# A decoder block with a grouped mixture of experts: h2 kept in natural column order, its first parts made later, slot weights by float32r products

## The chip, the cores and the metric

The kernel runs on one core of one Trainium2 chip. Its time is device microseconds for one execution of the whole program; several executions are made and the median counts. All tensors are float32 in HBM.

## The reference

One decoder layer on 256 tokens of 1024 columns. A mixing part (two kinds of attention, two gated branches, an output projection) makes a new residual `x`. Then a router picks for every token one group of four and two experts in it, out of 16 experts of width 512:

```python
h2 = rmsnorm(x, norm2_g[l]) * (1.0 + scale2) + shift2
...
g_prob = jax.nn.softmax((hf @ rg_w + rg_b).astype(jnp.float32), axis=-1)
g_top_p, g_idx = lax.top_k(g_prob, 1)
...
for e in range(N_EXPERTS):
    act = jax.nn.silu(hf @ w_gate[e]) * (hf @ w_up[e])
    out = out + combine[:, e:e + 1] * (act @ w_down[e])
```

The residual `x + gate2 * moe(h2)` is normalised once more and is the output.

## The kernel before

The mixing part fills the first half of the time; the change does not touch it. The second half works as follows.

**Router.** Tokens stand on partitions in two tiles `t` (128 tokens each), the 1024 columns in two halves `n`. `wo_steps` makes the output projection on TensorE, `x1_half(t, n)` turns one of its four quarters into the new residual (three VectorE operations, L947, L948 and L950) and sums squares on ScalarE (L949). `rstd2` makes the factor of the norm on GpSimd. `q_transpose` turns the tile (L956, copied by ScalarE, L957), `token_logits` multiplies it with the router's weights, `fold` copies the sums (L908) and adds them up, `weigh_logits` finishes the logits. Nineteen small VectorE and TensorE steps follow (`larger`, `place`, `selb`, the rank `rk`), `mod_rows(5)` puts two plain float32 products on TensorE, and `one_hot` writes, for each expert, a 0/1 matrix of 128 tokens by 64 slots.

**h2.** `h2_half` finishes h2 in place (L997). `h2_hi` rounds a half to float32r on ScalarE (L1009) and `h2_lo` takes the rest on VectorE (L1012); the pair of parts keeps float32 accuracy in float32r products. Both read h2 at every fourth column, because the expert weights lie in SBUF with rows `4p+k` on partition `p`: they read strided and write a permuted tile, whose 128 columns `k` stand together.

**Gather.** `gather(g, half)` runs once for each of the four groups: for eight column blocks `k`, the parts of h2 of two token tiles are the stationary operand (128x128) and the one-hot matrix of four experts (256 columns) is the moving one. That is 32 products for a group (L1200), in float32r.

**Experts.** Pairs `p` = 0 to 7. For a pair TensorE does gate and up products (`in_half`, L1240), then `slot_weights(p)`, then the down products of the pair before (`down_rows`, L1297) with `act_transpose` between their halves. `scatter_pair` (L1331) adds the result of pair `p-2` into the residual, with the transposed one-hot matrix `sT` as stationary operand. `slot_weights` before: two transposes of the one-hot matrix through TensorE (L1250), two plain float32 products with the combine weights (16 columns, L1252), a ScalarE copy of the transposed matrix (L1255) and two of the weights `ws` (L1258).

**Order.** In the router TensorE, VectorE and ScalarE run in the order in which the code is written (`manual_schedule`), and in the expert loop TensorE does. In the loop a scheduler sets the order on the other engines. The expert weights, some 100 MB, come over SyncE's queue into ring buffers; a load waits until the tile that had its buffer is used up.

Of the kernel before, what the change touches and what calls it, by code (L numbers as in the profile page):

```python
# [61 lines left out]
def hybrid_block_kernel(  # L62
# [931 lines left out]
    def h2_half(t, n):  # L994

        cs = slice(512 * n, 512 * n + 512)
        V.scalar_tensor_tensor(h2[t][:, cs], h2[t][:, cs], r2[t], adaacc[3, n], op0=ALU.mult,  # L997
                               op1=ALU.add)

    def h2_cols(t, n):  # L1000

        return h2[t][:, 512 * n:512 * n + 512].rearrange("t (p k) -> t k p", k=4)

    def h2_part(t, i, n):
        return h2s[t][i][:, 512 * n:512 * n + 512].rearrange("t (k p) -> t k p", k=4)

    def h2_hi(t, n):

        S.copy(h2_part(t, 0, n), h2_cols(t, n))  # L1009

    def h2_lo(t, n):
        V.tensor_tensor(h2_part(t, 1, n), h2_cols(t, n), h2_part(t, 0, n).bitcast(F32),  # L1012
                        op=ALU.subtract)

    def tok(t):
        return slice(t * P, (t + 1) * P)
# [13 lines left out]
    rstd2(0)  # L1030
    q_transpose(0, 0)
    h2_half(0, 0)
    h2_hi(0, 0)
    h2_lo(0, 0)
    wo_steps(1, ws, [(k, 1) for k in W3])
    q_transpose(0, 1)
    q_transpose(1, 0)
    token_logits(0)
    seed(0, 0)
    fold(tok(0), 0, "lgs0")  # L1040
    x1_half(1, 1)
    rstd2(1)
    q_transpose(1, 1)
    seed(0, 1)
    weigh_logits(0)
    h2_half(0, 1)
    h2_half(1, 0)
    token_logits(1)
    fold(tok(1), 32, "lgs1")
# [5 lines left out]
    seed(1, 0)  # L1055
    seed(1, 1)

    larger = moe.tile([P, SETS, 16], F32, name="larger", bufs=1)
    G.memset(larger, 0.0)

    def rt(shape, name, dt=F32):
# [126 lines left out]
    def gather(g, half):  # L1188

        if half == 0:  # L1190
            hgs[g] = late.tile([P, KD, 4 * CAP], F32, name="hg", tag="s8", bufs=2)
        hg, oh = hgs[g], onehot[g % 2]
        for k2 in range(2 * half, 2 * half + 2):
            ps = psa(f"hg{g}{k2}")
            for kk in range(2):
                k = 2 * k2 + kk
                n = 0
                for t in range(NT):
                    for i in range(2):
                        PE.matmul(ps[:, kk * T:(kk + 1) * T], h2s[t][i][:, k * P:(k + 1) * P],  # L1200
                                  oh[:, t].rearrange("p e s -> p (e s)"),
                                  start=(n == 0 and kk == 0), stop=(n == 3), skip_group_check=True)
                        n += 1
            S.copy(hg[:, 2 * k2:2 * k2 + 2, :], ps.rearrange("p (k s) -> p k s", k=2))
# [39 lines left out]
    def slot_weights(p):  # L1244

        lo = (2 * p) % 4
        oh = [onehot[p // 2 % 2][:, t, lo:lo + 2, :].rearrange("p e s -> p (e s)") for t in range(NT)]
        sp = psa(f"st{p}")
        for t in range(NT):
            PE.transpose(sp[:, t * P:(t + 1) * P], oh[t].bitcast(F32), ident)  # L1250
        for t in range(NT):
            PE.matmul(sp[:, T:T + NE], oh[t].bitcast(F32), combv[:, t, :], start=(t == 0),  # L1252
                      stop=(t == 1))
        sT = moe.tile([P, T], F32R, name="sT", tag="sT")
        S.copy(sT, sp[:, 0:T])  # L1255
        ws = moe.tile([P, 1], F32, name="ws", tag="ws")
        for i in range(2):
            S.copy(ws[64 * i:64 * i + 64, :],  # L1258
                   sp[64 * i:64 * i + 64, T + 2 * p + i:T + 2 * p + i + 1])
        sw[p] = ws, sT  # L1260

    def silu_up(p):
# [60 lines left out]
        V.tensor_tensor(yl, y, hi.bitcast(F32), op=ALU.subtract)  # L1323
        ys[p, FW * n] = hi, yl

    def scatter(yy, sT, n, cs):

        for y in yy:
            for t in range(NT):
                m = sT[:, t * P:(t + 1) * P]  # L1330
                PE.matmul(oacc[t][n][:, cs], m.bitcast(F32) if len(yy) == 1 else m, y, start=False,  # L1331
                          stop=True, skip_group_check=True)

    def scatter_pair(p, n, c):
        scatter(ys.pop((p, c.start)), sw[p][1], n, slice(c.start - FW * n, c.stop - FW * n))

    one_hot(0)
    for t in range(NT):
        h2_lo(t, 1)
    combv = route_weights()  # L1340
    by_hand.__exit__(None, None, None)
    NP = NE // 2
    whole_cols = [slice(0, FW), slice(FW, D)]
# [56 lines left out]
    with tc.If(nmaxv > CAP):  # L1400
        iota2 = small.tile([P, P], F32, name="iota2", tag="lgs")
        G.iota(iota2, pattern=[[1, P]], base=1, channel_multiplier=0,
               allow_small_or_imprecise_dtypes=True)
        with tc.For_i(0, NE, 1) as e:
            def load(w, name):
                hs = []
                for i in range(2):
                    h = w.shape[1] // 2
                    t_ = ring.tile([P, 2048], F32, name=f"{name}{i}", tag="ring")
                    k = h // P  # L1410
                    tv = t_.rearrange("p (k f) -> p k f", k=k)
                    src = w[bass.ds(e, 1), i * h:(i + 1) * h, :]
                    nc.sync.dma_start(tv, src.rearrange("a (p k) f -> p (a k) f", k=k) if k == 4 else
                                      src.rearrange("a (k p) f -> p (a k) f", p=P))
                    hs.append(tv)
                return hs
            gw, uw, dw = load(w_gate, "og"), load(w_up, "ou"), load(w_down, "od")
            pe_ = moe.tile([P, NT], F32, name="pe_")
            ce_ = moe.tile([P, NT], F32, name="ce_")
            for t in range(NT):  # L1420
                V.tensor_copy(pe_[:, t:t + 1], pos[:, t, bass.ds(e, 1)])
                V.tensor_copy(ce_[:, t:t + 1], combv[:, t, bass.ds(e, 1)])
            for r0 in (CAP, CAP + P):
                pr = moe.tile([P, NT], F32, name="pr")
                V.tensor_scalar(pr, pe_, float(-r0), None, op0=ALU.add)
                so = yhs[1][:, 0:NT * P].rearrange("p (t s) -> p t s", t=NT)
                for t in range(NT):
                    V.tensor_scalar(so[:, t, :], iota2, pr[:, t:t + 1], None, op0=ALU.is_equal)
                hq = late.tile([P, KD, P], F32, name="hq", tag="s8", bufs=2)
                for k in range(KD):  # L1430
                    ps = psa("ohg")
                    for n, (t, i) in enumerate(((0, 0), (0, 1), (1, 0), (1, 1))):
                        PE.matmul(ps[:, 0:P], h2s[t][i][:, k * P:(k + 1) * P], so[:, t, :],
                                  start=(n == 0), stop=(n == 3))
                    S.copy(hq[:, k, :], ps[:, 0:P])
                sp = psa("ost")
                for t in range(NT):
                    PE.transpose(sp[:, t * P:(t + 1) * P], so[:, t, :].bitcast(F32), ident)
                sT = moe.tile([P, T], F32R, name="osT", tag="sT")
                S.copy(sT, sp[:, 0:T])  # L1440
                wp = psa("owp")
                for t in range(NT):
                    PE.matmul(wp[:, 0:1], so[:, t, :].bitcast(F32), ce_[:, t:t + 1],
                              start=(t == 0), stop=(t == 1))
                ws = moe.tile([P, 1], F32, name="ows", tag="ws")
                V.tensor_copy(ws, wp[:, 0:1])
                gu = []
                for nm, hs in (("og", gw), ("ou", uw)):
                    ps = psa(f"{nm}ps")
                    for k in range(KD):  # L1450
                        PE.matmul(ps, hq[:, k, :], hs[k // 4][:, k % 4, :], start=(k == 0),
                                  stop=(k == KD - 1))
                    gu.append(ps)
                S.activation(act, gu[0], AF.Silu)
                V.tensor_tensor(act, act, gu[1], op=ALU.mult)
                ap = psa("oactT")
                for f in range(KF):
                    PE.transpose(ap[:, f * P:(f + 1) * P], act[:, f * P:(f + 1) * P], ident)
                aT = moe.tile([P, KF, P], F32, name="oaT", tag="aT")
                V.tensor_copy(aT, ap.rearrange("p (f s) -> p f s", f=KF))  # L1460
                for n in range(2):
                    cs = slice(512 * n, 512 * n + 512)
                    ps = psa("odps")
                    for f in range(KF):
                        PE.matmul(ps, aT[:, f, :], dw[f // 2][:, f % 2, cs], start=(f == 0),
                                  stop=(f == KF - 1))
                    scatter(weigh(ps, ws, n, slice(0, 512)), sT, n, slice(0, 512))
        for i in range(len(PARTS)):
            norm_part(i)
        norm_end()  # L1470
# [25 lines left out]
```

## Time and profile before

| | |
|---|---|
| median of 3 runs | 463.81 us (462.78 to 463.82) |
| the profiled execution | 462.77 us, of which the traced span is 460.8 us |
| TensorE matmul busy | 443.0 us (96%) |
| VectorE, ScalarE busy | 221.1 us (48%), 159.6 us (35%) |
| moved by DMA | 158.98 MB, mean 345 GB/s |
| granted TensorE clock, mean | 0.993 of full speed |

Busy time of TensorE is counted from modelled ends, so 96% does not mean that it multiplies at its peak. All rows below come from the profiled execution.

### The profile page before, as it was taken

How to read it: one execution, taken by the hardware profiler on the slowest of the kernel's cores; microseconds unless marked ns; L12 is line 12 of the kernel's file. 1: busy time of each engine (PE TensorE's matmuls, PEld its weight loads, DVE VectorE, ACT ScalarE, POOL GpSimd, SP SyncE). 2: the span in 40 equal slices, each digit the busy share in tenths (PEclk: the TensorE clock that was granted, in tenths of full speed). 3: DMA queues.
4: the chain of work that ended last, by engine and by line, in shares of the span. 5: the costliest groups of instructions: out<-in, count | busy, mean ns of one | idle time of the engine just before them, and what ended most of it. 6: DMA issues, size and time to landing. Idle time of an engine off the chain costs nothing.

```text
span 460.8 us, 6816 instructions
## 1 busy us (share of the span) xinstructions
PE 443.0 (96%) x2701; PEld 278.5 (60%) x2701; DVE 221.1 (48%) x380; ACT 159.6 (35%) x289; POOL 15.7 (3%) x52
## 2 busy tenths in 40 slices
PE   5999999999999999999899999999999999999992
PEld 1769888885888999977653335333543335333341
DVE  5557878956999974697570121020300202021133
ACT  3534596566574444364470102110210102011022
POOL 5200000000000000000100000000000000000000
PEclk9999999999999999999999999999999999999997
DMA  8999976799797969976798999999999999999922
GB/s 287 367 325 349 327 275 241 246 337 328 265 359 283 372 249 400 420 317 251 247 373 331 425 420 422 420 420 420 420 421 420 421 421 420 420 419 421 372 75 95
DMA packets 52099, 158.98 MB, mean 345 GB/s; under 512 B 6456, under 2 KB 16728, under 8 KB 40288
## 3 DMA queue, kind: packets, MB, share of 16 engines
q1 hardware_dynamic: 51856, 158.23, 89.4%
q8 instruction: 23, 0.38, 0.4%
q10 hardware_dynamic: 208, 0.28, 0.2%
q14 instruction: 12, 0.10, 0.1%
HBM read 157.45 MB, written 1.05 MB: 344 GB/s over the span
## 4 chain that ended last, share of the span: by engine, by line
PE 82%; DVE 9%; DMA 4%; issue 2%; ACT 1%; POOL 0%; SPq 0%; DVEq 0%; ACTq 0%
PE gps L1240 12%; PE ups L1240 12%; PE dps L1297 11%; PE g_acc L409 7%; PE wo L940 5%; PE br L878 4%; PE oacc L1331 4%; PE hg L1200 3%; PE qb_acc L409 2%; DMA adaw<-in_ada_w 2%; PE kb_acc L409 2%; DVE adarow L446 2%; PE ka_acc L409 2%; PE va_acc L401 2%; DMA u<-in_expert_w_up 2%
## 5 line engine op out<-in xcount | busy, mean ns | idle before, releaser
L1240 PE MATMUL gps<-g,hg 128*64 128x512 f32 x256 | 57.9, 597 | 0.0
L1240 PE MATMUL ups<-u,hg 128*64 128x512 f32 x256 | 56.6, 595 | 0.0
L1297 PE MATMUL dps<-d,aT 128*64 128x512 f32 x224 | 51.2, 599 | 0.0
L1269 DVE TENSOR_TENSOR act<-act,ups 128x512 f32<-128x512 f32 x8 | 5.5, 688 | 93.3 <-PE ups L1240 93.3
L409 PE MATMUL g_acc<-hT,wsp 128*128 128x256 f32 x384 | 48.4, 285 | 0.3 <-DVE wsp L363 0.3
L409 PEld LDWEIGHTS g_acc<-hT,wsp 128*128 128x128 f32 x384 | 46.7, 192 | 1.6 <-issue 1.0
L1240 PEld LDWEIGHTS ups<-u,hg 128*64 128x64 f32 x256 | 17.9, 137 | 35.3 <-issue 35.3
L1240 PEld LDWEIGHTS gps<-g,hg 128*64 128x64 f32 x256 | 17.4, 137 | 33.2 <-issue 32.3
L1297 PEld LDWEIGHTS dps<-d,aT 128*64 128x64 f32 x224 | 14.8, 136 | 25.3 <-issue 25.0
L446 DVE SCALAR_TENSOR_TENSOR adarow<-adaw,cact,adarow 128x512 f32<-128x512 f32 x40 | 29.7, 746 | 0.4
L1315 ACT CAST yh<-yt 128x512 fp32r<-128x512 f32 x15 | 9.3, 619 | 54.4 <-DVE yt L1311 54.4
L1255 ACT CAST sT<-st 128x256 fp32r<-128x256 f32 x8 | 3.0, 372 | 63.4 <-PE st L1252 63.4
L940 PE MATMUL wo<-wsp,mT 128*128 128x512 f32 x96 | 23.7, 401 | 0.7 <-DVE wsp L363 0.7
L1268 ACT ACTIVATE act<-gps 128x512 f32<-128x512 f32 x8 | 4.8, 598 | 54.0 <-PE gps L1240 54.0
L878 PE MATMUL br<-oT,wsp 128*128 128x256 f32 x192 | 23.2, 283 | 0.0
L878 PEld LDWEIGHTS br<-oT,wsp 128*128 128x128 f32 x192 | 23.0, 188 | 0.2 <-DVE wsp L363 0.2
L940 PEld LDWEIGHTS wo<-wsp,mT 128*128 128x128 f32 x96 | 17.7, 189 | 5.1 <-DVE wsp L363 1.1
L1323 DVE TENSOR_TENSOR yl<-yt,yh 128x512 fp32r<-128x512 f32 x7 | 4.8, 692 | 33.1 <-PE oacc L1331 32.4
L1276 DVE COPY aT<-actT 128x512 f32<-128x512 f32 x8 | 5.5, 692 | 27.6 <-PE actT L1274 27.6
L1311 DVE SCALAR_TENSOR_TENSOR yt<-dps,ws,adarow 128x512 f32<-128x512 f32 (+1 forms) x17 | 12.2, 719 | 12.0 <-PE dps L1297 8.3
L1200 PEld LDWEIGHTS hg<-onehot,h2s 128*128 128x128 f32 x128 | 15.6, 191 | 2.9 <-ACT yh L1315 2.4
L1200 PE MATMUL hg<-onehot,h2s 128*128 128x256 f32 x128 | 16.6, 288 | 0.0
(293 smaller groups left out, 671.5 us busy)
## 6 DMA issues: line engine op xcount, KB each, us to landing
g<-in_expert_w_gate SPq DMA_DIRECT2D x32, 1024.0 KB, 14.8
u<-in_expert_w_up SPq DMA_DIRECT2D x32, 1024.0 KB, 17.2
d<-in_expert_w_down SPq DMA_DIRECT2D x30, 1024.0 KB, 17.3
adaw<-in_ada_w SPq DMA_DIRECT2D x16, 1024.0 KB, 5.7
ada<-in_ada_w SPq DMA_DIRECT2D x8, 512.0 KB, 8.9
ada<-in_ada_w SPq DMA_DIRECT2D x16, 256.0 KB, 8.8
wo<-in_w_out SPq DMA_DIRECT2D x4, 1024.0 KB, 12.9
kaw<-in_w_in SPq DMA_DIRECT2D x4, 512.0 KB, 6.6
```

The costliest lines, as they stand in the source:

```text
L401: PE.matmul(self.acc[t], hT[b][:, k, t * P:(t + 1) * P], w[a][:, kk, :], start=(k == 0 and i == 0), stop=(k == KD - 1 and i == 2))
L409: PE.matmul(self.acc[m // 2][:, (m % 2) * T:(m % 2 + 1) * T], w[a][:, kk, m * P:(m + 1) * P], hT[b][:, k, :], start=(k == 0 and i == 0 and ...
L446: V.scalar_tensor_tensor(acc, adaw[which, j, k // 4][:, k % 4, :], cact[:, k:k + 1], acc, op0=ALU.mult, op1=ALU.add)
L878: PE.matmul(bacc[br][m // 2][:, (m % 2) * T:(m % 2 + 1) * T], wk[a][:, 0, m * P:(m + 1) * P], oT[br][b][:, k, :], start=(k == 0 and i == 0 ...
L940: PE.matmul(acc[t][n], mT[b][:, k, t * P:(t + 1) * P], ws[k // 2][a][:, k % 2, :], start=(k == 0 and i == 0), stop=(k == KD - 1 and i == 2))
L1200: PE.matmul(ps[:, kk * T:(kk + 1) * T], h2s[t][i][:, k * P:(k + 1) * P], oh[:, t].rearrange("p e s -> p (e s)"), start=(n == 0 and kk == 0 ...
L1240: PE.matmul(ps[64 * i:64 * i + 64, :], hg[:, k, (lo + i) * CAP:(lo + i + 1) * CAP], wt[nm, p][half][i][:, k % 4, :], start=(k == 0), stop= ...
L1269: V.tensor_tensor(av, av, in_place(gu["u", p]), op=ALU.mult)
L1297: PE.matmul(ys[p, FW * n][64 * i:64 * i + 64, :], aTs[p][:, 2 * h + k, 64 * i:64 * i + 64], dt_[p, h][i][:, k, FW * n:FW * n + FW], start= ...
L1311: V.scalar_tensor_tensor(y, ps, ws, adaacc[5, n][:, cs], op0=ALU.mult, op1=ALU.mult)
L1315: S.copy(hi, y)
L1331: PE.matmul(oacc[t][n][:, cs], m.bitcast(F32) if len(yy) == 1 else m, y, start=False, stop=True, skip_group_check=True)
```

## The change

Three edits, in code and in order:

1. `h2_hi` and `h2_lo` no longer permute: they read and write 512 neighbouring columns. The gather (and the overflow path, which does not run on these inputs) instead takes as stationary operand every fourth column of the float32r tile, a step of 16 bytes.
2. In the router `h2_hi(0, 0)` stands behind the first `fold` instead of ahead of the second part of `wo_steps`, and `h2_lo(0, 0)` behind `h2_half(0, 1)`.
3. `slot_weights` does two float32r products of 160 columns: the one-hot matrix is stationary, and the moving tile `wmove` holds the identity (128 columns) beside the high and low parts of one token tile's combine weights (32 columns). `wmove` is made once. The sum of the parts, `ws`, becomes two VectorE reductions. `sT` comes out with its token tiles swapped, so `scatter_pair` names the order.

```diff
     def h2_hi(t, n):
-        S.copy(h2_part(t, 0, n), h2_cols(t, n))
+        cs = slice(512 * n, 512 * n + 512)
+        S.copy(h2s[t][0][:, cs], h2[t][:, cs])
...
+    def h2_cols(t, i, k):
+        h, k = divmod(k, 4)
+        return h2s[t][i][:, 512 * h + k:512 * h + 512:4]
...
     h2_half(0, 0)
-    h2_hi(0, 0)
-    h2_lo(0, 0)
     wo_steps(1, ws, [(k, 1) for k in W3])
...
     fold(tok(0), 0, "lgs0")
+    h2_hi(0, 0)
     x1_half(1, 1)
...
     h2_half(0, 1)
+    h2_lo(0, 0)
     h2_half(1, 0)
...
-                        PE.matmul(ps[:, kk * T:(kk + 1) * T], h2s[t][i][:, k * P:(k + 1) * P],
+                        PE.matmul(ps[:, kk * T:(kk + 1) * T], h2_cols(t, i, k),
...
-        for t in range(NT):
-            PE.transpose(sp[:, t * P:(t + 1) * P], oh[t].bitcast(F32), ident)
-        for t in range(NT):
-            PE.matmul(sp[:, T:T + NE], oh[t].bitcast(F32), combv[:, t, :], start=(t == 0),
-                      stop=(t == 1))
+        PE.matmul(sp[:, 0:SW], oh[1], wmove[:, 2 * NE:2 * NE + SW], start=True, stop=True)
+        PE.matmul(sp[:, SW:2 * SW], oh[0], wmove[:, 0:SW], start=True, stop=True)
...
-            S.copy(ws[64 * i:64 * i + 64, :],
-                   sp[64 * i:64 * i + 64, T + 2 * p + i:T + 2 * p + i + 1])
+            V.tensor_reduce(ws[64 * i:64 * i + 64, :],
+                            sp[64 * i:64 * i + 64, P + 2 * p + i:P + 4 * NE:NE], axis=AX, op=ALU.add)
...
+    SW = P + 2 * NE
+    wmove = moe.tile([P, 2 * NE + SW], F32R, name="wmove", tag="wmove", bufs=1)
+    S.copy(wmove[:, 2 * NE:SW], ident)
+    for t in range(NT):
+        hi, lo = (wmove[:, SW * t + NE * i:SW * t + NE * i + NE] for i in range(2))
+        S.copy(hi, combv[:, t, :])
+        V.tensor_tensor(lo, combv[:, t, :], hi.bitcast(F32), op=ALU.subtract)
```

On ScalarE, in the router between the square sums of tile 0 and those of tile 1 (`wo_2445` and `wo_2446` are the two accumulators whose squares are summed, `qT` the transposed tiles, `lgs` the copy of the logits):

```order
 L949 ACTIVATE wo_2445,ss_2331<-xs 128x512
 L957 COPY qT<-qT_2495 128x4x128
-L1009 CAST h2s_2324<-h2a 128x512
-L957 COPY qT<-qT_2522 128x4x128
-L957 COPY qT<-qT_2528 128x4x128
-L908 COPY lgs_2544<-lgT 128x128
+L957 COPY qT<-qT_2520 128x4x128
+L957 COPY qT<-qT_2526 128x4x128
+L908 COPY lgs_2542<-lgT 128x128
+L1003 CAST h2s_2324<-h2a 128x512
 L949 ACTIVATE wo_2446,ss_2331<-xs 128x512
```

The rounding of the first part of h2 moves behind the logits' copy, and now stands right ahead of the square sum of tile 1.

On VectorE at the same place (`h2a` holds h2 of both token tiles, `h2s_2325` is the low part of tile 0):

```order
 L950 TENSOR_TENSOR h2a<-xs,adarow_1228 128x512
 L997 SCALAR_TENSOR_TENSOR h2a<-h2a,rstd_2491,adarow_1305 128x512
-L1012 TENSOR_TENSOR h2s_2325<-h2a,h2s_2324 128x512
 L947 TENSOR_TENSOR h2a<-wo_2446,adarow_793 128x512
 L948 TENSOR_TENSOR xs<-xs,h2a 128x512
```

The low part no longer stands ahead of `x1_half(1, 1)` (L947, L948, L950); it now comes two rows behind it, between the two `h2_half` of the other quarters.

On TensorE, in the pair p = 1 of the expert loop, between the last up products and the first down products (`u_1` and `d_0` are weight tiles), before:

```order
L1240 MATMUL ups_2802<-u_1_2773,hg 64x512
L1240 MATMUL ups_2802<-u_1_2775,hg 64x512
L1250 MATMUL st_2821<-ident,onehot_2613 128x128 x2
L1252 MATMUL st_2821<-rt_comb,onehot_2613 128x16 x2
L1297 MATMUL dps_0_2831<-d_0_2777,aT 64x512
L1297 MATMUL dps_0_2831<-d_0_2779,aT 64x512
```

and of the change:

```order
L1241 MATMUL ups_2806<-u_1_2777,hg 64x512
L1241 MATMUL ups_2806<-u_1_2779,hg 64x512
L1252 MATMUL st_2825<-wmove,onehot_2613 128x160
L1253 MATMUL st_2825<-wmove,onehot_2613 128x160
L1298 MATMUL dps_0_2833<-d_0_2781,aT 64x512
L1298 MATMUL dps_0_2833<-d_0_2783,aT 64x512
```

Four instructions of the program become two; their neighbours are the same.

## Rows read from the trace of the kernel before

**Rows 1.** The profile's page: span, busy time by engine, chain that ended last.

```profile
span 460.8 us, 6816 instructions
PE 443.0 (96%) x2701; PEld 278.5 (60%) x2701; DVE 221.1 (48%) x380; ACT 159.6 (35%) x289; POOL 15.7 (3%) x52
PE 82%; DVE 9%; DMA 4%; issue 2%; ACT 1%; POOL 0%; SPq 0%; DVEq 0%; ACTq 0%
```

**Rows 2.** Chain in order of time (start, us, what), from the router to the end.

```profile
234.12 1.83 PE bc L477 x4
235.95 3.82 PE hg L1200 x32
239.77 7.02 PE gps L1240 x32
...
262.21 6.87 PE ups L1240 x32
...
277.56 4.01 PE hg L1200 x32
...
430.98 3.58 PE dps L1297 x16
```

**Rows 3.** SyncE's queue over time, and, below, time from issue to landing (400 to 411).

```profile
401.57 7.79 SPq L206 DMA_DIRECT2D d<-in_expert_w_down  x4
...
d<-in_expert_w_down SPq DMA_DIRECT2D x4, 1024.0 KB, 19.8
```

**Rows 4.** Weight loads by shape: x count | busy us, mean ns.

```profile
L1240 PEld LDWEIGHTS ups<-u,hg 128*64 128x64 f32 x256 | 17.9, 137 | 35.3 <-issue 35.3
L1200 PEld LDWEIGHTS hg<-onehot,h2s 128*128 128x128 f32 x128 | 15.6, 191 | 2.9 <-ACT yh L1315 2.4 <-DVE onehot L1182 0.3 <-issue 0.2
```

**Rows 5.** ScalarE and VectorE groups by shape, contiguous ones and the strided L1009, L1012.

```profile
L1315 ACT CAST yh<-yt 128x512 fp32r<-128x512 f32 x15 | 9.3, 619 | 54.4 <-DVE yt L1311 54.4
L362 ACT CAST wsp<-wo 128x1024 fp32r<-128x1024 f32 x8 | 8.3, 1049 | 6.0 <-PE wo L940 6.0
L1009 ACT CAST h2s<-h2a 128x512 fp32r<-128x512 f32 x4 | 4.3, 1125 | 2.4 <-DVE h2a L997 2.4
L363 DVE TENSOR_TENSOR wsp<-wo,wsp 128x1024 fp32r<-128x1024 f32 x8 | 9.7, 1222 | 2.2 <-ACT wsp L362 2.2
L1318 DVE TENSOR_TENSOR yl<-yt,yh 128x512 fp32r<-128x512 f32 x8 | 5.5, 692 | 5.9 <-ACT yh L1315 5.9
L1012 DVE TENSOR_TENSOR h2s<-h2a,h2s 128x512 fp32r<-128x512 f32 x4 | 4.3, 1093 | 1.2 <-ACT h2s L1009 1.2
```

**Rows 6.** Timeline of the router (start, us, engine, line, what), 220 to 234.

```profile
220.68 4.43 PE L940 MATMUL wo<-wsp,mT 128*128 128x512 f32 x18
...
225.76 1.11 DVE L1012 TENSOR_TENSOR h2s<-h2a,h2s 128x512 fp32r<-128x512 f32 x1 [1.19 <-ACT h2s L1009]
...
226.76 0.27 ACT L908 COPY lgs<-lgT 128x128 f32<-128x128 f32 x1
226.78 0.69 DVE L947 TENSOR_TENSOR h2a<-wo,adarow 128x512 f32<-128x512 f32 x1
...
228.76 0.19 ACT L949 ACTIVATION_READ_ACCUMULATOR wo<-xs 128x1 f32 x1
...
230.54 0.75 DVE L997 SCALAR_TENSOR_TENSOR h2a<-h2a,rstd,adarow 128x512 f32<-128x512 f32 x1 [0.81 <-POOL rstd L250]
231.26 0.29 DVE L908 COPY lgs<-lgT 128x128 f32<-128x128 f32 x1
...
233.88 0.10 PEld L1084 LDWEIGHTS <-strictb 128*128 128x128 bf16 x1 [0.90 <-DVE rt_selb L1079]
```

**Rows 7.** Timeline around the slot weights of pair 1, 269 to 270.

```profile
269.01 0.20 PEld L1250 LDWEIGHTS st<-ident,onehot 128*128 128x128 f32 x2 [0.81 <-issue]
...
269.18 0.53 PEld L1252 LDWEIGHTS st<-rt_comb,onehot 128*128 128x128 f32 x4
...
269.73 0.20 PEld L1297 LDWEIGHTS dps<-d,aT 128*64 128x64 f32 x4
```

More of the change, by code (lines that the diff above doesn't have):

```diff
@@ L998, in h2_half @@
                                op1=ALU.add)
[L1000 to L1005, printed above, removed]
     def h2_hi(t, n):
-        S.copy(h2_part(t, 0, n), h2_cols(t, n))
+        cs = slice(512 * n, 512 * n + 512)
+        S.copy(h2s[t][0][:, cs], h2[t][:, cs])
     def h2_lo(t, n):
-        V.tensor_tensor(h2_part(t, 1, n), h2_cols(t, n), h2_part(t, 0, n).bitcast(F32),
+        cs = slice(512 * n, 512 * n + 512)
+        V.tensor_tensor(h2s[t][1][:, cs], h2[t][:, cs], h2s[t][0][:, cs].bitcast(F32),
                         op=ALU.subtract)
+    def h2_cols(t, i, k):
+        h, k = divmod(k, 4)
+        return h2s[t][i][:, 512 * h + k:512 * h + 512:4]
     def tok(t):
@@ L1056, in hybrid_block_kernel @@
     seed(1, 1)
-    larger = moe.tile([P, SETS, 16], F32, name="larger", bufs=1)
+    larger = moe.tile([P, 192], F32, name="larger", tag="wmove", bufs=1)
+    larger = larger[:, 0:SETS * 16].rearrange("p (s c) -> p s c", s=SETS)
     G.memset(larger, 0.0)
@@ L1248, in slot_weights @@
         sp = psa(f"st{p}")
-        for t in range(NT):
-            PE.transpose(sp[:, t * P:(t + 1) * P], oh[t].bitcast(F32), ident)
-        for t in range(NT):
-            PE.matmul(sp[:, T:T + NE], oh[t].bitcast(F32), combv[:, t, :], start=(t == 0),
-                      stop=(t == 1))
+        PE.matmul(sp[:, 0:SW], oh[1], wmove[:, 2 * NE:2 * NE + SW], start=True, stop=True)
+        PE.matmul(sp[:, SW:2 * SW], oh[0], wmove[:, 0:SW], start=True, stop=True)
         sT = moe.tile([P, T], F32R, name="sT", tag="sT")
-        S.copy(sT, sp[:, 0:T])
+        S.copy(sT.rearrange("p (t s) -> p t s", t=NT),
+               sp[:, 0:384].rearrange("p (t c) -> p t c", t=NT)[:, :, 0:P])
         ws = moe.tile([P, 1], F32, name="ws", tag="ws")
         for i in range(2):
-            S.copy(ws[64 * i:64 * i + 64, :],
-                   sp[64 * i:64 * i + 64, T + 2 * p + i:T + 2 * p + i + 1])
+            V.tensor_reduce(ws[64 * i:64 * i + 64, :],
+                            sp[64 * i:64 * i + 64, P + 2 * p + i:P + 4 * NE:NE], axis=AX, op=ALU.add)
         sw[p] = ws, sT
@@ L1324, in weigh_low, with scatter @@
         ys[p, FW * n] = hi, yl
-    def scatter(yy, sT, n, cs):
+    def scatter(yy, sT, n, cs, order=(0, 1)):
         for y in yy:
             for t in range(NT):
-                m = sT[:, t * P:(t + 1) * P]
+                m = sT[:, order[t] * P:(order[t] + 1) * P]
                 PE.matmul(oacc[t][n][:, cs], m.bitcast(F32) if len(yy) == 1 else m, y, start=False,
@@ L1334, in scatter_pair @@
     def scatter_pair(p, n, c):
-        scatter(ys.pop((p, c.start)), sw[p][1], n, slice(c.start - FW * n, c.stop - FW * n))
+        scatter(ys.pop((p, c.start)), sw[p][1], n, slice(c.start - FW * n, c.stop - FW * n),
+                (1, 0))
     one_hot(0)
@@ L1432, in hybrid_block_kernel @@
                     for n, (t, i) in enumerate(((0, 0), (0, 1), (1, 0), (1, 1))):
-                        PE.matmul(ps[:, 0:P], h2s[t][i][:, k * P:(k + 1) * P], so[:, t, :],
+                        PE.matmul(ps[:, 0:P], h2_cols(t, i, k), so[:, t, :],
                                   start=(n == 0), stop=(n == 3))
```

## Prediction

> **What bounds the kernel now.** I began with the page: TensorE's matmuls are busy 96% of the span, and the chain of work that ended last lies 82% on TensorE [rows 1]. The chain in order of time shows that in the second half it hardly leaves TensorE: the two plain float32 products of `mod_rows`, 32 gather products in 3.82 us, 32 gate products, and so on through the pairs, each piece starting where the one before ends [rows 2]. So here a nanosecond more or less on TensorE is one in the end time, unless something else arrives later still.
>
> The candidate for that is the weight stream. The last whole down tiles (pair 6) are issued between 401.57 and 409.4 us and land 19.8 us later, so by about 429.2 [rows 3]; the first half of them is wanted at 430.98 [rows 2], and the second half, which is the one that lands by 429.2, only after that half's 3.58 us and the transposes, at 435. The first half is issued in the first half of the stretch, so by 405.5, and lands by 425.3. TensorE could come some 5.5 us earlier before it would wait there. Coming later costs the stream nothing.
>
> Then I read three places by themselves: the gather's weight loads, the router's timeline, and the gap between up and down products.
>
> **Change, part by part.**
>
> *Gather, strided stationary operand.* The number of products stays (4 groups x 32 = 128), and so do their sizes; only the column step of the stationary operand goes from 4 to 16 bytes. No row of before has a stationary operand with such a step, so the price needs bounds. First the loads as they are: a 64-column load takes 137 ns, a 128-column one 191 [rows 4], so a column costs 54/64 = 0.84 ns beside some 83 fixed, and the 128 columns 108 ns. The gather makes one product per 4.01/32 = 125 ns [rows 2]. Loads thus fill nearly the whole pace already, though they run beside the products: there is only 17 ns of room per product.
>
> What does a step of 16 bytes do to a reader? The only rows with it are those of the copies that the change takes away. ScalarE needs 619 ns for 512 columns and 1049 for 1024 that are contiguous, 0.84 ns each and 189 fixed, the same pace as the weight load's. With the step it needs 1125 for 512, so (1125 - 189)/512 = 1.83 ns each. VectorE goes from 1.04 ns (692 for 512, 1222 for 1024) to (1093 - 162)/512 = 1.82 [rows 5]. Two engines of different pace come out at the same 1.82 ns when every element lies in another 16 bytes. That looks like a limit on the memory's side and not on the engine's, and it is why I take it for TensorE's loads too, ScalarE's row being the nearest: same step, same pace before. A load's columns then take 128 x 1.82 = 233 ns instead of 108, longer than the product beside it, and set the pace. If the 17 ns of room swallow part of it the pace is 233, and the loss (233 - 125) x 128 = 13.8 us; if the 17 ns stay on top, 250 and 16.0 us. I take 14.9. The lower bound is nothing (the load doesn't feel the step); between them lies VectorE's ratio, 1093/692 = 1.58 on 108 ns, +63 ns and 8.0 us. All four gathers lie on the chain, so nothing hides this.
>
> The Trainium skill, "SBUF — State Buffer" (Door 1: The DMA port swizzle), says that SBUF has 16-byte lines and that full bandwidth needs at least two accesses to a line. Rows 5 agree for ScalarE and VectorE; no run here shows it for TensorE. If I read it as two column times for each single access, a load's columns would take 215 ns by the row's 0.84, and the sum below would be 2.3 us lower, an estimate.
>
> *Contiguous copies.* ScalarE saves 4 x 506 ns, VectorE 4 x 401 ns [rows 5]. Only the pair for quarter (0, 0) was on a path (next item). The others run beside `mod_rows` and the first half of the gather, so I count them as nothing; if that cover were gone they would be worth at most 3 x 0.9 = 2.7 us, a gain.
>
> *Router order.* Tile 1's last accumulation ends at 220.68 + 4.43 = 225.11. VectorE could take it up then, but `h2_lo(0, 0)` runs from 225.76 to 226.87 and L947 starts at 226.78 [rows 6]. Without it the three operations of `x1_half(1, 1)` come 1.6 us earlier. That is the upper bound. What is late next is ScalarE: the moved rounding now stands ahead of the square sum. The logits' copy ends at 227.03; 0.62 for the rounding, about 0.6 for the square sum of as many columns and 0.19 for reading it end near 228.45, where before it was 228.95. From there to `h2_half(1, 0)` on VectorE it took 1.59 us (228.95 to 230.54), and the copy of tile 1's logits is queued behind that, at 231.26 [rows 6]. So the copy comes 0.5 us earlier, and with it the logits, the rank at 233.88 and the gather. `h2_lo(0, 0)`, now 0.69 us, fits into VectorE's wait for that factor (0.81 before). I take -0.5; the lower bound is 0, should the factor's chain not move.
>
> *Slot weights.* From the first load of `st` to the first load of `dps` TensorE spends 269.73 - 269.01 = 0.72 us [rows 7]. The last of the six loads starts at 269.18 + 0.53 - 0.19 = 269.52, so 0.21 is the wait from it to the next tile shape. After: two float32r products of 160 columns. Nearest row: the gather, 125 ns for 256 columns with a 128-column load. 2 x 0.125 + 0.21 = 0.46, a gain of 0.26. It counts for pairs 1 to 7; in pair 0 the next TensorE work is the transpose of `act`, which waits for VectorE. 7 x 0.26 = 1.8 us; I take -2.0 since 160 columns are fewer than 256. The other bound: if 160 columns go at the plain float32 pace (7.02 us for 32 products of 512 columns, two side by side [rows 2], so 0.44 for 512, two passes), 2 x 2 x 0.14 + 0.21 = 0.77, a loss of 0.3 in all.
>
> *The rest costs nothing.* `wmove` is one cast of 128 columns, two of 16 and two small subtractions, some 1 us on ScalarE and VectorE, hidden by 7.02 us of gate products and 6.9 of up products from 239.77 on, ahead of its first use [rows 2]; uncovered, 1 us once. The 16 copies for `ws` become 16 reductions on VectorE, which is 48% busy over the span [rows 1] and far less here. They wait for `st`; queued behind them is the copy of the transposed `act`, which is wanted only 3.58 us of down products later. Uncovered they would be 0.3 us a pair.
>
> **Sum.** +14.9 - 0.5 - 2.0 = +12.4 us. On the profiled execution (462.77) that is 475.2. That execution lies 1.0 us under the median of the runs (463.81), on which it is 476.2. I say 475.7.
>
> **The rivals.** *A, as above: loads feel the step.* With VectorE's ratio and the best of the gains (8.0 - 1.6 - 2.0) +4.4 and 467.2; with 16.0 and no gains +16.3 and 480: its own range is 467 to 480.
>
> *B, loads don't feel it.* Every load row depends on its column count alone (137 and 191 ns), and the load might be fed early enough by a queue that runs ahead. Then only the gains remain: -2.5, so 460.3 to 461.3, down to 459.9 with a further part of the router's 1.6. The weight stream has 5.5 us of room and stays hidden. It decides at a pace of 125 + 2500/128 = 145 ns a product: below it the kernel is faster. For it: TensorE is not ScalarE, its loads have a path of their own beside the products. Against it: the common 1.82 ns of two engines. The Trainium skill, "TensorE: Matmul & The Clock Gate" (LDWEIGHTS), gives a load's time by its column count alone, which is B; rows 4 agree for contiguous columns, and no row of before shows another step.
>
> *C, B with the products of 160 columns at the plain pace:* the slots give nothing, 0.3 us are lost, -0.5 remains in the router, 462.6 to 463.6, no change.
>
> **Chances.** A 62%, B 29%, C 9%. What a measurement of this kernel can tell from no change is about 0.3%, 1.4 us. A is slower in all its range, B faster, C the same. The range has to leave out at most 2 in 10: from the bottom of B, 459.9, to 479.
>
> **What would show it.** A: gather products at 230 to 250 ns, each gather near 7.6 to 8 us on the chain instead of 4.0, and longer weight loads than 191 ns in its group; B: 125 ns and 4.0 us. Slots: 0.45 us from the first load of `st` to `dps`; 0.7 would be C. Router: the rank's load about 0.5 us earlier than 233.88, square sum of tile 1 behind the rounding. The prediction is wrong if the load's reader is not held by the lines that hold ScalarE and VectorE; the rest moves 3 us at most.

## The result, and the profile after

The changed kernel takes 475.12 us (median of 4 runs, 474.2 to 475.33), the one before 463.81: a ratio of 1.0246, 95% interval 1.0226 to 1.0265. It is slower, by 11.3 us. The single times of one kernel lie mostly in two clusters some 1.1 us apart (before: about 462.8 and 463.9), and two executions, one of the kernel before at 2491.37 us and one of router_only at 892.83, are left out as slow; so small differences are read below from traced spans as well as from medians.

The profiled execution of the change takes 474.2 us. Its page, span and busy time by engine:

```profile
span 472.5 us, 6759 instructions
PE 453.9 (96%) x2669; PEld 289.5 (61%) x2669; DVE 222.2 (47%) x398; ACT 156.9 (33%) x276; POOL 16.1 (3%) x52
```

Beside [rows 1] there are fewer instructions, and both TensorE rows are 11 us longer, as the span is (11.7). The chain in order of time (start, us, what) says where:

```profile
233.80 1.83 PE bc L477 x4
235.62 7.35 PE hg L1201 x32
242.97 7.02 PE gps L1241 x32
...
265.42 6.87 PE ups L1241 x32
272.67 3.58 PE dps L1298 x16
...
280.42 7.67 PE hg L1201 x32
...
337.08 7.67 PE hg L1201 x32
...
393.75 7.67 PE hg L1201 x32
```

Against [rows 2] gate, up and down products take what they took; the gathers take 7.35 and three times 7.67 us in place of 3.82, 4.01 and these two of the kernel before:

```profile
331.29 4.01 PE hg L1200 x32
385.01 4.02 PE hg L1200 x32
```

Together that is 14.5 us more. It exceeds the whole loss; the other parts gave some of it back. The groups of the lines that the change touched (busy us, mean ns of one | idle before):

```profile
L1201 PEld LDWEIGHTS hg<-onehot,h2s 128*128 128x128 f32 x128 | 30.2, 328 | 2.8 <-ACT yh L1316 2.4 <-DVE onehot L1183 0.2
...
L1007 DVE TENSOR_TENSOR h2s<-h2a,h2s 128x512 fp32r<-128x512 f32 x4 | 2.7, 686 | 0.0
...
L1003 ACT CAST h2s<-h2a 128x512 fp32r<-128x512 f32 x4 | 2.3, 617 | 2.0 <-DVE h2a L997 2.0
```

A load of the same 128x128 tile takes 328 ns where it took 191 [rows 4], and the copies that lost their step went from 1125 and 1093 ns [rows 5] to 617 and 686. The weight-load unit on the timeline inside the second gather, a window of one us of the change, and then of the kernel before:

```profile
280.80 1.50 PEld L1201 LDWEIGHTS hg<-onehot,h2s 128*128 128x128 f32 x6
```

```profile
278.42 1.27 PEld L1200 LDWEIGHTS hg<-onehot,h2s 128*128 128x128 f32 x10
```

Taking one load's own time off the stretch leaves the distance from load to load: (1.50 - 0.33)/5 = 0.234 us after, (1.27 - 0.19)/9 = 0.120 before. The 0.234 is 128 columns at the 1.82 ns that the prediction worked out of [rows 5].

Around the slot weights of pair 1 (timeline, 272 to 273):

```profile
272.21 0.19 PEld L1252 LDWEIGHTS st<-wmove,onehot 128*128 128x128 f32 x1 [0.81 <-issue]
...
272.60 0.20 PEld L1298 LDWEIGHTS dps<-d,aT 128*64 128x64 f32 x4
```

0.39 us from the first load to that of `dps`, 0.72 before [rows 7]. The router's timeline, to be laid beside [rows 6]; the last `wo` products run from 220.86 here, so everything stands 0.18 us later than there before the change can act:

```profile
220.86 4.43 PE L940 MATMUL wo<-wsp,mT 128*128 128x512 f32 x18
...
226.89 0.27 ACT L908 COPY lgs<-lgT 128x128 f32<-128x128 f32 x1
227.05 0.62 ACT L1003 CAST h2s<-h2a 128x512 fp32r<-128x512 f32 x1
227.57 0.61 ACT L949 ACTIVATE wo<-xs 128x512 f32<-128x512 f32 x1
228.10 0.19 ACT L949 ACTIVATION_READ_ACCUMULATOR wo<-xs 128x1 f32 x1
...
228.40 1.20 POOL L249 TENSOR_SCALAR rstd<-ss,rstd 128x1 f32<-128x1 f32 x1 [4.26 <-ACT wo L949]
228.86 0.69 DVE L1007 TENSOR_TENSOR h2s<-h2a,h2s 128x512 fp32r<-128x512 f32 x1
230.28 0.75 DVE L997 SCALAR_TENSOR_TENSOR h2a<-h2a,rstd,adarow 128x512 f32<-128x512 f32 x1 [0.73 <-POOL rstd L250]
230.95 0.28 DVE L908 COPY lgs<-lgT 128x128 f32<-128x128 f32 x1
```

The rounding stands ahead of the square sum, the square sum ends at 228.29, and tile 1's logits are copied at 230.95: 0.31 earlier by the clock of the trace, 0.49 against the start of the stretch.

### The profile page after: what moved, and what is told of

The parts are those of the page before. It is cut to its first block, busy times and chain, and to the rows that moved or that the text cites. A ratio compares the mean times of both kernels' runs of the same rounds, so it can differ in the third digit from the quotient of the medians.

```text
span 472.5 us, 6759 instructions
## 1 busy us (share of the span) xinstructions
PE 453.9 (96%) x2669; PEld 289.5 (61%) x2669; DVE 222.2 (47%) x398; ACT 156.9 (33%) x276; POOL 16.1 (3%) x52
## 4 chain that ended last, share of the span: by engine, by line
PE 81%; DVE 9%; DMA 4%; issue 2%; ACT 1%; SPq 1%; POOL 0%; DVEq 0%; ACTq 0%
PE gps L1241 12%; PE ups L1241 12%; PE dps L1298 11%; PE g_acc L409 7%; PE hg L1201 6%; PE wo L940 5%; PE br L878 4%; PE oacc L1332 4%; PE vb_acc L401 2%; PE qb_acc L409 2%; PE kb_acc L409 2%; DMA ada<-in_ada_w 2%; DVE adarow L446 2%; DMA qaw<-in_w_in 2%; PE dps L1286 2%
## 5 line engine op out<-in xcount | busy, mean ns | idle before, releaser
L1201 PEld LDWEIGHTS hg<-onehot,h2s 128*128 128x128 f32 x128 | 30.2, 328 | 2.8 <-ACT yh L1316 2.4
L1201 PE MATMUL hg<-onehot,h2s 128*128 128x256 f32 x128 | 31.1, 401 | 0.0
## 6 DMA issues: line engine op xcount, KB each, us to landing
g<-in_expert_w_gate SPq DMA_DIRECT2D x32, 1024.0 KB, 14.5
```

What stands on the lines that cost most here:

```text
L1201: PE.matmul(ps[:, kk * T:(kk + 1) * T], h2_cols(t, i, k), oh[:, t].rearrange("p e s -> p (e s)"), start=(n == 0 and kk == 0), stop=(n == 3 ...
```

## The experiments

The theory: the 16-byte step of the stationary operand slows the loads, since a load fetches one 16-byte line in 1.82 ns and the step puts every element into a line of its own. Rivals: something else in the change (order, copies, slot weights) made the gather slow, or any step other than 4 bytes does so.

**blocks.** The change with the old column blocks in the gather, all else kept.

```diff
     def h2_cols(t, i, k):
-        h, k = divmod(k, 4)
-        return h2s[t][i][:, 512 * h + k:512 * h + 512:4]
+        return h2s[t][i][:, k * P:(k + 1) * P]
```

> The changed kernel, except that the gather reads 128 neighbouring columns (step 4 bytes) again while the copies stay in natural order; so it gathers other columns than the weights want, and its numbers are not the layer's. Theory (the step of 16 bytes makes a weight load's columns take 1.82 ns each and sets the gather's pace): gather products back at 125 ns, about 4.0 us a group, and 14.5 us less than the changed kernel's 475.1, so 460.6. Rival (part of the loss comes from elsewhere, the moved copies or the slot products): more than 462.

460.58 us (459.93 to 460.66) against 463.89 of the kernel before on that chip, ratio 0.9927 (0.9905 to 0.995). The gather's loads and its first two pieces on the chain:

```profile
L1200 PEld LDWEIGHTS hg<-onehot,h2s 128*128 128x128 f32 x128 | 15.6, 191 | 2.9 <-ACT yh L1315 2.4 <-issue 0.2 <-DVE onehot L1182 0.2
```

```profile
235.60 3.82 PE hg L1200 x32
276.87 4.02 PE hg L1200 x32
```

Its span is 458.2, 14.3 us under that of the change. The step, alone, turns a gain into the loss.

**step8B, step12B, step32B.** The same products with steps of 2, 3 and 8 columns; each line replaces the body of `h2_cols`.

```diff
-        return h2s[t][i][:, 512 * h + k:512 * h + 512:4]
+        return h2s[t][i][:, 256 * b + k:256 * b + 256:2]
...
+        return h2s[t][i][:, 512 * h + k:512 * h + k + 382:3]
...
+        return h2s[t][i][:, k:D:8]
```

> The changed kernel with the gather reading every second column (a step of 8 bytes), so it gathers other columns than the weights want. Theory (one 16-byte line per 1.82 ns): 64 lines a load, 117 ns, no longer than the 125 ns of a product as it was; gather pace 125 to 130 ns, time 460.6 to 461.3. Rival (any step other than one column halves the load's speed): pace about 215 to 233 ns, time 472 to 475.

> The changed kernel with the gather reading every third column (a step of 12 bytes), other columns than the weights want. Theory (one 16-byte line per 1.82 ns): 96 lines a load, 175 ns a product, 5.6 us a group, time about 467. Rival (any step halves the speed): 233 ns, 475. Second rival (only a step of 16 bytes or more costs): 125 ns, 460.6.

> The changed kernel with the gather reading every eighth column (a step of 32 bytes), other columns than the weights want. Theory (every column another 16-byte line, whatever the distance): 233 ns a product, the time of the changed kernel, 475. Rival (the price grows with the distance, by 32-byte or larger units): above 233 ns, up to 450, and up to 500 us.

Medians 460.18, 467.74 and 476.0 us; ratios 0.9922 (0.9894 to 0.9949), 1.0087 (1.0053 to 1.012), 1.0263 (1.0234 to 1.0292). The weight loads in a window of one us inside the second gather, of step8B, step12B and step32B in this order:

```profile
277.34 1.27 PEld L1201 LDWEIGHTS hg<-onehot,h2s 128*128 128x128 f32 x10
```

```profile
278.79 1.31 PEld L1201 LDWEIGHTS hg<-onehot,h2s 128*128 128x128 f32 x7
```

```profile
281.85 1.31 PEld L1200 LDWEIGHTS hg<-onehot,h2s 128*128 128x128 f32 x5
```

With the mean load of each (196, 263 and 338 ns, from its group) the distance from load to load is 0.119, 0.174 and 0.243 us. 128 columns 8 bytes apart touch 64 lines, 12 bytes apart 96, 16 or 32 bytes apart 128; at 1.82 ns a line that is 0.117, 0.175 and 0.233. So 8 bytes cost nothing because 0.117 is still under the pace of 0.120 that contiguous loads have, 12 bytes cost in proportion, and beyond 16 bytes there is little more to lose: 32 bytes take 4% more than the count of lines gives, which stays unexplained. A limit that starts with any step is out.

**slots_only.** Only edit 3 of the change.

```diff
-        for t in range(NT):
-            PE.transpose(sp[:, t * P:(t + 1) * P], oh[t].bitcast(F32), ident)
...
+        PE.matmul(sp[:, 0:SW], oh[1], wmove[:, 2 * NE:2 * NE + SW], start=True, stop=True)
+        PE.matmul(sp[:, SW:2 * SW], oh[0], wmove[:, 0:SW], start=True, stop=True)
```

> The kernel before with the third edit alone (slot weights by two float32r products of 160 columns, sums on VectorE). Theory: 0.39 us from the first load of st to dps where it was 0.72, in seven pairs, so -2.3 us: 461.5. Rival (the gain is lost again because the new reductions on VectorE or the making of wmove hold something up, or the weight stream becomes the bound): 463 to 464.

460.86 us (460.25 to 461.7) against 463.9, ratio 0.994 (0.9918 to 0.9961); span 458.6 against 460.8, 2.2 us. On the chain the two products are

```profile
269.16 0.27 PE st L1250
269.43 0.11 PE st L1251
```

so the second one of 160 columns adds 0.11 us: the pace of the float32r gather, not that of plain float32. The rival's 463 to 464 is out.

**router_only.** Only edit 2: the moved calls, with the strided copies of before.

```diff
-    h2_hi(0, 0)
-    h2_lo(0, 0)
     wo_steps(1, ws, [(k, 1) for k in W3])
...
     fold(tok(0), 0, "lgs0")
+    h2_hi(0, 0)
...
     h2_half(0, 1)
+    h2_lo(0, 0)
```

> The kernel before with the second edit alone: h2_hi(0, 0) behind the first fold, h2_lo(0, 0) behind h2_half(0, 1), both still permuting (1.13 and 1.09 us). Theory (the square sum of tile 1 waits for the rounding ahead of it on ScalarE): the longer rounding ends near 228.2, the square sum at 228.95 as before, so no gain: 463.8, within 0.2. Rival (the gain of 0.3 to 0.5 us came from VectorE starting x1_half(1, 1) early): 463.3.

464.38 us against 463.88, ratio 1.0019 (0.9998 to 1.0041): not told from no change, and its single times spread from 462.56 to 467.19. In its trace `wo` starts 0.38 us later than in [rows 6], so 0.38 has to be taken off what follows before it is compared:

```profile
221.06 4.43 PE L940 MATMUL wo<-wsp,mT 128*128 128x512 f32 x18
...
228.81 0.20 ACT L949 ACTIVATION_READ_ACCUMULATOR wo<-xs 128x1 f32 x1
...
229.07 1.09 DVE L1012 TENSOR_TENSOR h2s<-h2a,h2s 128x512 fp32r<-128x512 f32 x1
229.12 1.13 POOL L249 TENSOR_SCALAR rstd<-ss,rstd 128x1 f32<-128x1 f32 x1 [4.78 <-ACT wo L949]
...
230.93 0.75 DVE L997 SCALAR_TENSOR_TENSOR h2a<-h2a,rstd,adarow 128x512 f32<-128x512 f32 x1 [0.76 <-POOL rstd L250]
231.59 0.28 DVE L908 COPY lgs<-lgT 128x128 f32<-128x128 f32 x1
```

Tile 1's logits are copied at 231.59 - 0.38 = 231.21, and before at 231.26: the order alone gives nothing. VectorE starts `x1_half(1, 1)` 1.6 us earlier, as in the change. The longer strided rounding, which now stands ahead of the square sum, takes 1.3 of that: the square sum is read off at 229.01 - 0.38 = 228.63, against 228.95 before. The other 0.3 goes in the factor's chain, which from there to `h2_half(1, 0)` takes 1.92 us instead of 1.59; GpSimd's step L249 in it ends at 230.25, just behind VectorE's strided low part (to 230.16). So the theory had the time right, but the square sum did not stay at 228.95.

The trace then loses time further on. TensorE around the fold, and the engines by stretch (PE busy, PEld, DVE, ACT, POOL, granted clock, DMA share, GB/s):

```profile
231.93 0.40 PE L910 MATMUL lgp<-fold,lgs 128*128 128x20 f32 x2 [1.80 <-DVE lgs L908]
232.18 3.50 PE L986 MATMUL oacc<-xs,ident 128*128 128x512 f32 x4
235.47 0.22 PE L1084 MATMUL rk<-rt_selb,strictb 128*128 128x16 bf16 x1
```

```profile
228.00:232.00 4.00, 2.20 (x26) 1.17 (x24) 2.98 (x6) 1.77 (x5) 1.69 (x2) 1.00 0.92 340
232.00:236.00 4.00, 4.00 (x10) 1.81 (x11) 3.19 (x13) 2.86 (x3) 0.00 (x0) 0.57 1.00 414
```

TensorE stood idle for 1.80 us ahead of that fold, and in the stretch behind it the granted clock was 0.57 on average, so most of it went by at the lower level of 1.2 GHz; the four `oacc` products took 3.50 us there and 1.96 before (from 231.85). From the logits' copy to the rank it took 3.88 us, against 2.62 in [rows 6]. Of its executions the two longest (467.2 us) had a mean granted clock of 0.986, the shortest (462.56) one of 0.995. The change itself has 1.36 us of idle time at the same place, and its clock there is 1.00:

```profile
232.00:236.00 4.00, 3.93 (x14) 1.98 (x13) 3.83 (x16) 1.65 (x4) 0.00 (x0) 1.00 1.01 420
```

**lo_late.** Another order: the rounding stays where it was, and only `h2_lo(0, 0)` moves, behind `x1_half(1, 1)`.

```diff
     h2_hi(0, 0)
-    h2_lo(0, 0)
...
     x1_half(1, 1)
+    h2_lo(0, 0)
     rstd2(1)
```

> The kernel before with h2_lo(0, 0) alone moved, behind x1_half(1, 1); h2_hi(0, 0) stays where it was. Theory (VectorE's low part held x1_half(1, 1) up by 1.6 us, and with no rounding ahead of it the square sum follows at once): the copy of tile 1's logits 1.0 us earlier, 462.8. Rival (GpSimd's factor or TensorE sets the pace there): less than 0.3 us, 463.6.

462.89 us, ratio 0.9982 (0.9967 to 0.9998): a gain, of 0.2%. In the trace the copy of the logits comes at 230.16, and the gather starts at 234.84 in place of 235.95:

```profile
227.15 1.08 DVE L1012 TENSOR_TENSOR h2s<-h2a,h2s 128x512 fp32r<-128x512 f32 x1
227.41 0.19 ACT L949 ACTIVATION_READ_ACCUMULATOR wo<-xs 128x1 f32 x1
...
227.71 0.60 POOL L249 TENSOR_SCALAR rstd<-ss,rstd 128x1 f32<-128x1 f32 x1 [3.80 <-ACT wo L949]
...
230.16 0.28 DVE L908 COPY lgs<-lgT 128x128 f32<-128x128 f32 x1
```

With no rounding ahead of it the square sum is read off at 227.60, 1.35 us earlier than before, and 1.1 of that reaches the gather, as the theory had it.

**permuted_write.** The kernel before, with the copies reading contiguous columns and writing them 512 bytes apart.

```diff
     def h2_cols(t, n):
-        return h2[t][:, 512 * n:512 * n + 512].rearrange("t (p k) -> t k p", k=4)
+        return h2[t][:, 512 * n:512 * n + 512].rearrange("t (p k) -> t p k", k=4)
```

(`h2_part` changes in the same way.)

> The kernel before, with the same permuting copies walked in the other order: they read neighbouring columns and write with a step of 512 bytes. The result is the same. Theory (the limit of one line per 1.82 ns holds for reading): if writing has no such limit the copies take 0.62 and 0.69 us as contiguous ones do, and VectorE's x1_half(1, 1) starts 0.4 us earlier: 463.3 to 463.5. Rival (writing has the same limit): copies stay at 1.13 and 1.09 us (the VectorE copy also reads the high part with a step), 463.8.

463.82 us, ratio 1.0006 (0.9991 to 1.002). The copies' groups:

```profile
L1009 ACT CAST h2s<-h2a 128x512 fp32r<-128x512 f32 x4 | 4.0, 1098 | 2.4 <-DVE h2a L997 2.4
L1012 DVE TENSOR_TENSOR h2s<-h2a,h2s 128x512 fp32r<-128x512 f32 x4 | 4.2, 1082 | 1.2 <-ACT h2s L1009 1.2
```

1098 and 1082 ns, 2% and 1% under [rows 5]: the rival came in. ScalarE's copy only writes with a step here, so for it scattered writes cost what scattered reads cost. VectorE's copy also reads the high part with that step, so its 1082 does not show what the writes alone cost.

**pairs, pairs_lo, slots_lo_late.** If two elements of a line are as good as four, the permutation can be split: the copies move pairs of columns (8 bytes), and the gather takes every second column. `pairs` is the change with this, `pairs_lo` has the order of lo_late as well, and `slots_lo_late` is lo_late with the slot weights of the change, permuting in the copies as before.

```diff
+    def pairs(ap, by_p):
+        how = "t (p j c) -> t j p c" if by_p else "t (j p c) -> t j p c"
+        return ap.rearrange(how, j=2, c=2)
...
-        S.copy(h2s[t][0][:, cs], h2[t][:, cs])
+        S.copy(pairs(h2s[t][0][:, cs], 0), pairs(h2[t][:, cs], 1))
...
-        h, k = divmod(k, 4)
-        return h2s[t][i][:, 512 * h + k:512 * h + 512:4]
+        b, k = divmod(k, 2)
+        return h2s[t][i][:, 256 * b + k:256 * b + 256:2]
```

> The changed kernel with the permutation split in two: the copies move pairs of neighbouring columns (two of the four columns of a 16-byte line at a time), and the gather reads every second column. The result is the layer's. Theory (a line may be left after two accesses without loss): gather at 125 ns a product, copies at 0.62 to 0.70 us as contiguous ones, 14.5 us less than the changed kernel, so 460.6. Rival (a step anywhere in the copies' pattern costs): copies at 1.1 us, 461 to 461.5.

> The kernel of the run pairs, with h2_hi(0, 0) back at its old place (ScalarE waits there anyway) and h2_lo(0, 0) behind x1_half(1, 1). Theory (in the changed kernel the square sum of tile 1 waits behind the rounding): the copy of tile 1's logits comes another 0.5 to 0.6 us earlier, 460.0. Rival: no difference from the run pairs.

> The kernel before with the third edit and with h2_lo(0, 0) behind x1_half(1, 1); no strided gather. Theory: the two gains add up, -2.4 to -3.0 and -1.0, so 460.0 to 460.5. Rival (they share a cover, or the weight stream becomes the bound): 461 or more.

459.78, 459.78 and 460.01 us against 463.94; ratios 0.9906 (0.988 to 0.9933), 0.9908 (0.9879 to 0.9937), 0.991 (0.988 to 0.9941); spans 458.0, 457.2 and 457.4. All three are faster than both kernels, by 0.9% than the one before, and the medians don't tell them apart. They don't show the 0.5 to 0.6 us that `pairs_lo` was expected to gain over `pairs`, but they fall in different clusters: four of six times of `pairs` lie at 459.74 to 459.79 and four of `pairs_lo` at 459.76 to 459.93, where the other cluster of `pairs` is at 460.7 and that of `pairs_lo` at 458.92. In the traces, one execution of each, the copy of tile 1's logits is at 230.64 in `pairs` and at 229.99 in `pairs_lo`, and the span is 0.8 us shorter. In `pairs`:

```profile
L1206 PEld LDWEIGHTS hg<-onehot,h2s 128*128 128x128 f32 x128 | 15.7, 195 | 2.9 <-ACT yh L1321 2.4 <-DVE onehot L1188 0.2 <-issue 0.2
...
L1011 DVE TENSOR_TENSOR h2s<-h2a,h2s 128x512 fp32r<-128x512 f32 x4 | 2.7, 684 | 0.0
L1007 ACT CAST h2s<-h2a 128x512 fp32r<-128x512 f32 x4 | 2.5, 666 | 1.9 <-DVE h2a L997 1.9
```

Loads and copies both run close to their contiguous durations (191, 686 and 617 ns). For ScalarE the lines say 189 + 256 x 1.82 = 655, and it took 666. So the permutation costs next to nothing if it is split between the copy and the load; ScalarE's copy is the one that still pays, 8%.

**moving16B.** The kernel before with the gather's moving operand strided by 16 bytes, to see whether the other input of a product is slowed too.

```diff
                         PE.matmul(ps[:, kk * T:(kk + 1) * T], h2s[t][i][:, k * P:(k + 1) * P],
-                                  oh[:, t].rearrange("p e s -> p (e s)"),
+                                  h2s[t][i][:, k % 4:D:4],
```

> The kernel before with the gather's moving operand replaced: 256 columns of the h2 part with a step of 16 bytes instead of the one-hot matrix, so the gathered rows are not the layer's. Theory (the limit of one line per 1.82 ns is the memory's, and holds for the moving operand too): 466 ns a product, 14.9 us a group, about 507 us. Rival (it holds for weight loads alone): 125 ns a product and 463.

One run, 478.56 us. The second gather on the chain, and its products on the timeline, a window of one us:

```profile
282.59 7.64 PE hg L1200 x32
```

```profile
283.75 1.58 PE L1200 MATMUL hg<-h2s 128*128 128x256 f32 x6
```

With 0.41 us for one product, (1.58 - 0.41)/5 = 0.234 us from product to product: 256 columns at 0.91 ns. It is slowed, but to half of what a load pays per column. Both operands come from the same tile in this run, and nothing here separates that from the step. Neither expectation (466 ns, or 125 as before) was met.

## Why the prediction was right

The forecast was 475.2 on the profiled execution (474.2 came) and 475.7 overall (475.12 came). The sum of +12.4 us was 1.1 too high against the medians (+11.3), and 475.7 comes nearer than that because it was set midway between the sum on the profiled execution and on the median (476.2).

*Gather, +14.9 predicted, +14.5 measured.* The mechanism was rival A as written: a load feels the step, and the line takes 1.82 ns, as on ScalarE and VectorE. Two small errors met. The pace of before was taken as 4.01/32 = 125 ns, which has the start of a gather in it; from load to load it was 120. And of the two paces after, 233 and 250, the lower one came, so the whole fixed part of a load lies beside the one before. (234 - 120) x 128 = 14.6, and the chain gives 14.5.

The Trainium skill, "TensorE: Matmul & The Clock Gate" (LDWEIGHTS), has a load's time follow from its column count alone. That was rival B, and it fell: the same 128 columns took 191, 196, 263, 328 and 338 ns by their step. The Trainium skill, "SBUF — State Buffer" (Door 1: The DMA port swizzle), asks for two accesses to a 16-byte line for full bandwidth. By that rule the traces agree, for TensorE's loads too: two elements to a line ran at the contiguous pace, one did not.

*Router, -0.5 predicted, -0.5 measured,* by two errors that cancel, which is luck. The square sum was read off at 228.29 - 0.18 = 228.11 on the clock of [rows 6], 0.34 earlier than the 228.45 forecast: the forecast put ScalarE's operations end to end, and in the trace each starts before the record of the one before it ends (the rounding at 227.05, the copy's end at 227.16). But the factor's chain from there to `h2_half(1, 0)` took 1.99 us and not the 1.59 counted on. GpSimd's step (L249) spans 1.20 us after and 0.80 before:

```profile
229.06 0.80 POOL L249 TENSOR_SCALAR rstd<-ss,rstd 128x1 f32<-128x1 f32 x1 [5.10 <-ACT wo L949]
```

In the change it ends at 229.60, just behind VectorE's low part (L1007, to 229.55). "Fits into VectorE's wait" was therefore too easy: VectorE had the time, but GpSimd, whose factor it waits for, seems to have been held meanwhile. The Trainium skill, "SBUF — State Buffer" (SBUF: two separate sides), says that VectorE and GpSimd share a port pair that is locked for a whole instruction, among others by a VectorE operation with two SBUF inputs against a GpSimd one that reads SBUF. By that, the low part, which has two such inputs, holds L249 until it ends, and the trace agrees (229.55 and 229.60). It agrees in router_only too (230.16 and 230.25) and in lo_late (228.23 and 228.31); no run was made to take it apart. What the change gained in this place came from the copies without a step: router_only shows the same order with strided copies to gain nothing, lo_late that another order gains 1.1.

*Slots, -2.0 predicted, -2.3 measured* (7 x 0.33): 160 columns take less than the 125 ns of the nearest row, as assumed, and rival C is out by slots_only.

*The rest at nothing:* blocks has the new copies, `wmove` and the reductions, and its span of 458.2 is 2.6 us under that of before, by 2.3 from the slots and 0.35 from the gather's start; nothing else shows. The three terms and the 0.18 us that the trace of after started late make 14.5 - 0.5 - 2.3 + 0.2 = 11.9, against 11.7 in the spans.

## What to carry to other kernels

A permutation can be paid in a copy off the critical path or in an operand of TensorE on it; before moving it, count the 16-byte lines that each reader then touches (here 1.82 ns a line for copies and weight loads) and compare with the pace that the instruction has anyway. Two float32 elements to a line cost weight loads and VectorE nothing here and ScalarE 8%, so a permutation by four splits into a pair move and a step of two. Where work is moved in a chain of several engines, look at whom it stands ahead of now: the strided rounding before the square sum took away 1.3 of the 1.6 us that the new order gave VectorE, and the rest was lost where GpSimd's step ended only behind the low part.

## What the runs showed of the hardware beyond that

- On ScalarE, writes 512 bytes apart cost about what reads 16 bytes apart cost (1098 ns against 1125).
- The moving operand paid 0.91 ns a column at a 16-byte step, half of the weight load's 1.82 (one run, both operands in one tile).
- GpSimd's one-column step L249 takes 0.27 us for tile 0 (at 223.05 in the change), and for tile 1, where VectorE's operations of 512 columns run, 0.32 to 1.20: it ends 0.05 to 0.14 us after one of them in the traces of before, the change, router_only, pairs, lo_late and pairs_lo. In the last two, where it is shortest (0.60 and 0.32), the step behind it, L250, takes 1.06 and 1.08 us in place of 0.56.
- In router_only, an idle stretch of 1.80 us on TensorE was followed by the lower clock; 1.36 us in the change were not. One trace each, so this is a coincidence that was seen, not a cause that was shown.
